# Gate and up of a SwiGLU FFN: blocks without 1/rms, one direct chunk, sums of weights half by accumulating DMAs

## The chip, the cores and the metric

One core of one Trainium2 chip. The metric is the device time of one execution in microseconds (us). TensorE (PE) multiplies, VectorE (DVE) and ScalarE (ACT) work on SBUF and PSUM elementwise, GpSimd (POOL) and SyncE (SP) mostly issue DMAs here. Each engine executes its own instructions in order and waits at semaphores for the others.

## The reference

One layer of a streaming encoder, 512 tokens, D = 1024, float32. Three token mixers run beside each other on one input projection and are merged with gates; then come the output projection, a residual addition, and an FFN of width 2816:

```python
h = rms_norm(x, norm_mix)                      # then mixers, gates, branch projections -> merged
x = x + merged @ w_out
h2 = rms_norm(x, norm_ffn)                     # x * rsqrt(mean(x*x) + 1e-6) * norm_ffn
act = silu(h2 @ w_ffn_gate) * (h2 @ w_ffn_up)  # 1024 -> 2816, twice
x = x + act @ w_ffn_down                       # 2816 -> 1024
```

The change concerns `h2`, gate and up. 1/rms is one factor per token, so it can be multiplied into `h2` or into the results of the two projections.

## The kernel before

**Products in three passes.** Activations lie transposed, channels on the 128 partitions and tokens along the row. Each float32 operand is split into hi and lo: ACT copies it to a rounded type (`whi`, `wh`), DVE subtracts (`wlo`, `wl`). A product is hi x hi + hi x lo + lo x hi, three matmuls. Split tiles of weights come from a pool with three buffers for each name, so a tile's buffer comes free when the product three back has been read. `make_a` prepares the split of a weight tile up to three products ahead.

**Direct chunks.** The first two of the 11 chunks of 256 columns of gate and up (`NDIRECT = 2`) multiply `h2` (all 512 tokens at once) directly: 96 matmuls of 512 columns per chunk. `h2` at that point has norm_ffn's gain but no 1/rms; `rb2`, the vector of 1/rms for all tokens, is multiplied in behind the matmuls. `rms2` computes it, with two matmuls of PE against a matrix of ones (`ps_rms2`).

**Chunks of seven products.** The other nine chunks (`seven`) take the four blocks of `h2` (two halves of the channels, two halves of the tokens) and the four blocks of a chunk's weights, and need seven block products for eight. A product has 24 matmuls of 256 columns. The blocks of `h2` are prepared while the direct chunks run: `norm2` multiplies gain and `rb2` in, `diff_b` makes the differences T1 to T4, `split_b` splits all seven. For each chunk DVE makes four sums of weight blocks (`sums_a`, L1385): S3 = 11 - 21, S2 = 22 - S3, S1 = 21 + 22, S4 = 12 - S2. The products run in `ORDER`, and accumulate in the PSUM tiles Y (`ps_y`) and X (`ps_x`); ACT takes snapshots of the accumulating halves into `tx` and `ty` (L1455). `finish_act` adds the last parts (L1430), takes Silu of the gate half, and multiplies (L1432) into `act`.

**Offsets.** `split_a` lays the first four weight tiles of the stage at the offsets 0, 4, 8 and 12 of their buffers (`STEPS`), all later ones at 16 (`OFF`).

**Down.** The FFN's last projection starts with four direct pieces (`ps_d`, weights `wlo`), then goes on in products of 256 columns into `ps_dy` and `ps_dx`. Its first activation blocks (`Bd11..`, `Bd12..`) are split by `split_d2` in part behind the last gate and up products. Its weights are `wld`: the names at the start of the stage are `wld<-dw` for the first five tiles and `wld<-dr` for the next ones. Some `dw` are sums, made by DMAs of POOL that accumulate in SBUF.

**Order.** A tile scheduler orders each engine's instructions. Some are pinned (`keep_in_program_order`), others moved ahead (`high_priority`).

Of the kernel before, what the change touches and what calls it, by code (L numbers as in the profile page):

```python
# [16 lines left out]
P = 128  # L17
# [12 lines left out]
NDIRECT = 2  # L30
# [37 lines left out]
def layer_kernel(ctx: ExitStack, tc: tile.TileContext, x, xt, vecs, w_in, w_qkv7, w_gate7, w_pool, w_rg, w_ig,  # L68
                 w_branch, w_br7, w_out, w_fg, w_fu, w_fd, w_fd7, out):
# [181 lines left out]
    for c in range(NDIRECT):  # L251
        add_chunk256(("fg", c), w_fg, c * 256)
        add_chunk256(("fu", c), w_fu, c * 256)
# [1002 lines left out]
    with ExitStack() as ffn:  # L1256
# [17 lines left out]
        h2 = []  # L1274
        for c in range(4):
            xr = g4([2, S], f"xr{c}")
            nc.sync.dma_start(xr, xt[2 * c * P:(2 * c + 2) * P, :].rearrange("(j p) t -> p j t", p=P))
            if c == 0:
                psh = [chunk_psum(("out", n), fp) for n in range(2)]
                for half in range(2):  # L1280
                    for n in range(2):
                        half_chunk(psh[n], ("out", n), half, mt, 0, n == half == 0)
            pss = psh[c] if c < 2 else chan_chunk(("out", c), mt, pool=fp)
            hh = g4([2, S], f"h2h{c}", F32R)
            hl = g4([2, S], f"h2l{c}", F32R)
            for j in range(2):
                k = 2 * c + j
                if c % 2 == 0:
                    x1p[c // 2, j] = mp.tile([P, 2, S], F32, tag="m", name=f"x1{c}{j}")
                t = x1p[c // 2, j][:, c % 2, :]  # L1290
                dve.tensor_tensor(t, pss[j], xr[:, j, :], ALU.add)
                x1.append(t)
                gcol = vcol("norm_ffn", k)
                act(hh[:, j, :], t, AF.Copy, scale=gcol)
                dve.scalar_tensor_tensor(hl[:, j, :], t, gcol, hh[:, j, :].bitcast(F32), ALU.mult,
                                         ALU.subtract)
                h2.append((hh[:, j, :], hl[:, j, :]))
                if k == 0:
                    act(sqsum, t, AF.Square)
                else:  # L1300
                    sq = small(f"sq2{k}", 2, "sq2")
                    act(sq, t, AF.Square)
                    dve.tensor_tensor(sqsum, sqsum, sq, ALU.add)

        def rms2():
# [5 lines left out]
            nc.tensor.matmul(ps, onesr, sh, start=True, stop=False)  # L1311
            nc.tensor.matmul(ps, onesr, sl, start=False, stop=True)
# [26 lines left out]
        def split_b(nm, key, which=0):  # L1339
            h, l = g4([4, H], f"B{which}{nm}h", F32R), g4([4, H], f"B{which}{nm}l", F32R)  # L1340
            act(h, BN[key], AF.Copy)
            dve.tensor_tensor(l, BN[key], h.bitcast(F32), ALU.subtract)
            B[which, nm] = h, l

        def diff_b(nm, x, y):
            BN[nm] = corner([4, H], f"hn{nm}")
            dve.tensor_tensor(BN[nm], BN[x], BN[y], ALU.subtract)

        def prepare_b():
            nrm = [lambda k=k: norm2(k) for k in range(8)]  # L1350
            return nrm[:4] + [lambda: split_b("11", (0, 0))] + nrm[4:] + [
                lambda: split_b("21", (1, 0)),
                lambda: diff_b("T1", (0, 1), (0, 0)),
                lambda: diff_b("T2", (1, 1), "T1"),
                lambda: split_b("T2", "T2"),
                lambda: split_b("T1", "T1"),
                lambda: diff_b("T3", (1, 1), (0, 1)),
                lambda: split_b("T3", "T3"),
                lambda: split_b("22", (1, 1)),
                lambda: diff_b("T4", (1, 0), "T2"),  # L1360
                lambda: split_b("T4", "T4")]

        SUMS = {"S2": (("S3", "11", "21", ALU.subtract), ("S2", "22", "S3", ALU.subtract)),
                "S1": (("S1", "21", "22", ALU.add),),
                "S4": (("S4", "12", "S2", ALU.subtract),)}
# [5 lines left out]
        made = [0, NDIRECT]  # L1371
        offs = []

        def load_a(c):
            for nm in ("11", "21", "22", "12"):
                raw[c, nm] = t = corner([2, 4, P], f"w{c}_{nm}")
                for w in range(2):
                    nc.sync.dma_start(t[:, w], cols((w_fg, w_fu)[w], KH[nm] * 4, 4, c * 256 + CH[nm] * P, P))

        def sums_a(c, nm):  # L1380
            for s_, x, y, op in SUMS.get(nm, ()):
                if (c, s_) in raw:
                    continue
                raw[c, s_] = t = wp.tile([P, 2, 4, P], F32, tag="raw", name=f"w{c}_{s_}")
                dve.tensor_tensor(t, raw[c, x], raw[c, y], op)  # L1385

        def make_a(upto):
            while made[0] < min(upto, len(steps)):
                c, nm = steps[made[0]]
                made[0] += 1  # L1390
                if (c, nm) == (NDIRECT, "11"):
                    offs.extend(STEPS)
                while made[1] < min(c + 2, DOWN):
                    load_a(made[1])
                    made[1] += 1
                sums_a(c, nm)
                A[c, nm] = split_a(raw[c, nm], f"{c}_{nm}")
# [30 lines left out]
        def finish_act(t, ps, a):  # L1428

            dve.tensor_tensor(t, t, ps, ALU.add)  # L1430
            act(t[:, 0, :], t[:, 0, :], AF.Silu)
            dve.tensor_tensor(a, t[:, 0, :], t[:, 1, :], ALU.mult)  # L1432


        PRE = ("S2", "S1", "S3")

        def seven(c):
            a = g4([2, S], f"act{c}")
            tx, ty = g4([2, S], f"tx{c}"), g4([2, S], f"ty{c}")
            Y = fp.tile([P, 2, S], F32, tag="mm", name=f"ps_y{c}")  # L1440
            X = fp.tile([P, 2, S], F32, tag="mm", name=f"ps_x{c}")
            lo, hi = slice(0, H), slice(H, S)
            plan = (("11", Y, 1, True, tx, lo, Y, hi),
                    ("12", X, 0, True, None, None, None, None),
                    ("S2", Y, 1, False, tx, hi, Y, hi),
                    ("S1", X, 1, False, ty, hi, X, hi),
                    ("S3", Y, 1, False, ty, lo, Y, hi),
                    ("S4", X, 1, False, None, None, None, None),
                    ("22", Y, 0, False, None, None, None, None))
            n0 = steps.index((c, "11"))  # L1450
            for n, (nm, ps, half, first, t, ts_, src, ss) in enumerate(plan):
                make_a(n0 + n + 3)
                product(A.pop((c, nm)), B[0, WITH[nm]], ps, half, first, True)
                if t is not None:
                    act(t[:, :, ts_], src[:, :, ss], AF.Copy)  # L1455
                if c == DOWN - 1 and nm in PRE:
                    split_d2("11", PRE.index(nm), 0, 0)
                if nm == "S4":
                    finish_act(tx, X, a[:, 0, :])
                if nm == "22":  # L1460
                    finish_act(ty, Y, a[:, 1, :])
            acts.append(a)

        bg.extend([lambda: None, rms2] + prepare_b())
        for c in range(NDIRECT):
            pg = chan_chunk(("fg", c), h2, 3, fp)
            pu = chan_chunk(("fu", c), h2, 3, fp)
            if c == NDIRECT - 1:
                make_a(3)
            a = g4([2, S], f"act{c}")  # L1470
            for j in range(2):
                sg = small(f"sg{c}{j}", 2, "sq2")
                dve.tensor_tensor(sg, pg[j], rb2, ALU.mult)
                act(sg, sg, AF.Silu)
                dve.tensor_tensor(sg, sg, pu[j], ALU.mult)
                dve.tensor_tensor(a[:, j, :], sg, rb2, ALU.mult)
            acts.append(a)
        tick(len(bg))
        for c in range(NDIRECT, NF // 2):
            if c == NF // 2 - 1:  # L1480
                ah, al = g4([2, S], "ah", F32R), g4([2, S], "al", F32R)
# [210 lines left out]
```

## Time and the profile before

| What | Value |
|---|---|
| Time, median of 3 runs | 898.24 us (898.1 to 898.4) |
| The profiled execution | 898.31 us, span 896.5 us |
| Input projection, mixers, branches, to the output projection | 0 to about 524 us |
| Output projection | about 524 to 570.6 us |
| Gate and up | 570.6 to 786.6 us |
| Down | 786.6 to 896 us |
| PE busy | 891.2 us, 99% of the span |
| DVE busy | 739.4 us, 82% |
| ACT busy | 528.5 us, 59% |
| POOL busy | 88.8 us, 10% |
| TensorE clock granted | 9 or more tenths in every slice but the last, 8 |

A row of a timeline gives start, length, engine, line, operation, out<-in, tile shape, and in brackets how long the engine was idle before and what it waited for. A row of groups gives count, busy time, mean ns, and idle time before. Lines of before and after have different numbers for the same place.

### The profile page before, as it was taken

How to read it: one execution, taken by the hardware profiler on the slowest of the kernel's cores; microseconds unless marked ns; L12 is line 12 of the kernel's file. 1: busy time of each engine (PE TensorE's matmuls, PEld its weight loads, DVE VectorE, ACT ScalarE, POOL GpSimd, SP SyncE). 2: the span in 40 equal slices, each digit the busy share in tenths (PEclk: the TensorE clock that was granted, in tenths of full speed). 3: DMA queues.
4: the chain of work that ended last, by engine and by line, in shares of the span. 5: the costliest groups of instructions: out<-in, count | busy, mean ns of one | idle time of the engine just before them, and what ended most of it. 6: DMA issues, size and time to landing. Idle time of an engine off the chain costs nothing.

```text
span 896.5 us, 14227 instructions
## 1 busy us (share of the span) xinstructions
PE 891.2 (99%) x5563; PEld 795.2 (89%) x5563; DVE 739.4 (82%) x934; ACT 528.5 (59%) x730; POOL 88.8 (10%) x130
## 2 busy tenths in 40 slices
PE   9999999999999999999999999999999999999998
PEld 6888778788889888888888988889999999999998
DVE  6897897997786599967887695699988888899974
ACT  6554989546856556554664544545555555746642
POOL 1110002222323101000001100000000000021200
PEclk9999999999999999999999999999999999999999
DMA  9495336798692785734636865336443343897913
GB/s 337 141 297 167 118 114 215 217 302 252 174 276 72 217 252 175 236 108 152 205 90 154 179 190 170 106 107 169 126 131 104 95 118 97 228 243 195 186 42 118
DMA packets 116644, 154.08 MB, mean 172 GB/s; under 512 B 8161, under 2 KB 90081, under 8 KB 116577
## 3 DMA queue, kind: packets, MB, share of 16 engines
q1 hardware_dynamic: 103904, 107.30, 37.8%
q0 software_dynamic: 12528, 45.62, 21.6%
q8 instruction: 43, 0.70, 0.3%
q10 hardware_dynamic: 144, 0.26, 0.1%
q14 instruction: 25, 0.20, 0.1%
HBM read 132.71 MB, written 18.87 MB: 169 GB/s over the span
## 4 chain that ended last, share of the span: by engine, by line
PE 95%; DVE 2%; ACT 2%; issue 1%; DMA 0%; SPq 0%; DVEq 0%; ACTq 0%
PE ps_y L287 11%; PE ps_x L287 8%; PE ps_q L798 7%; PE ps_dy L1611 6%; PE ps_dx L1611 5%; PE ps_br L278 3%; PE ps_br L279 3%; PE ps_br L280 3%; PE ps_bY L1238 2%; PE ps_gate L701 2%; PE ps_gy L287 2%; PE ps_gate L280 2%; PE ps_bX L1238 2%; PE ps_gx L287 2%; PE ps_gate L278 2%; PE ps_gate L279 2%
## 5 line engine op out<-in xcount | busy, mean ns | idle before, releaser
L111 ACT ACTIVATE whi<-raw 128x1024 fp32r<-128x1024 f32 x69 | 73.1, 1060 | 85.2 <-PE ps_out L279 17.9
L112 DVE TENSOR_TENSOR wlo<-raw,whi 128x1024 fp32r<-128x1024 f32 x69 | 84.4, 1223 | 30.7 <-ACT whi L111 30.7
L112 DVE TENSOR_TENSOR wlo<-qw,whi 128x1024 fp32r<-128x1024 f32 x48 | 58.6, 1224 | 22.0 <-ACT whi L111 21.8
L111 ACT ACTIVATE whi<-qw 128x1024 fp32r<-128x1024 f32 x48 | 50.7, 1059 | 33.2 <-PE ps_q L798 15.3
L1403 ACT ACTIVATE wh_S<-w_S 128x1024 fp32r<-128x1024 f32 x36 | 38.3, 1067 | 34.4 <-PE ps_y L287 22.3
L1404 DVE TENSOR_TENSOR wl_S<-w_S,wh_S 128x1024 fp32r<-128x1024 f32 x36 | 43.8, 1222 | 5.2 <-ACT wh_S L1403 5.1
L1515 POOL DMA_DIRECT2D dw<-in_w_down_dram x20 | 16.9, 847 | 313.6 <-DMA dw<-in_w_down_dram 253.2
L1403 ACT ACTIVATE wh<-w 128x1024 fp32r<-128x1024 f32 x27 | 28.8, 1067 | 30.2 <-issue 11.9
L1404 DVE TENSOR_TENSOR wl<-w,wh 128x1024 fp32r<-128x1024 f32 x27 | 33.0, 1222 | 9.9 <-ACT wh L1403 9.9
L1403 ACT ACTIVATE whdS<-dw 128x1024 fp32r<-128x1024 f32 x20 | 21.3, 1067 | 22.5 <-PE ps_dy L1611 11.0
L1404 DVE TENSOR_TENSOR wldS<-dw,whdS 128x1024 fp32r<-128x1024 f32 x20 | 24.3, 1226 | 6.5 <-ACT whdS L1403 6.4
L1054 DVE TENSOR_TENSOR_SCAN E<-K,ahead 128x512 f32<-128x512 f32 (+3 forms) x32 | 25.4, 815 | 4.4 <-ACT K L1050 4.4
L278 PE MATMUL ps_br<-yHH,whi 128*128 128x512 f32 x64 | 25.3, 395 | 0.0
L278 PE MATMUL ps_lru<-HH,whi 128*128 128x512 f32 x64 | 25.2, 394 | 0.0
L278 PE MATMUL ps_br<-yph,whi 128*128 128x512 f32 x64 | 25.2, 394 | 0.0
L278 PE MATMUL ps_pool<-HH,whi 128*128 128x512 f32 x64 | 25.2, 393 | 0.0
L280 PE MATMUL ps_gate<-HH,wlo 128*128 128x512 f32 x64 | 25.0, 391 | 0.0
L278 PE MATMUL ps_gate<-HH,whi 128*128 128x512 f32 x64 | 25.0, 391 | 0.0
L279 PE MATMUL ps_br<-ypl,whi 128*128 128x512 f32 x64 | 25.0, 391 | 0.0
L280 PE MATMUL ps_br<-yph,wlo 128*128 128x512 f32 x64 | 25.0, 391 | 0.0
L279 PE MATMUL ps_br<-yHL,whi 128*128 128x512 f32 x64 | 25.0, 390 | 0.0
L279 PE MATMUL ps_pool<-HL,whi 128*128 128x512 f32 x64 | 25.0, 390 | 0.0
(737 smaller groups left out, 3448.5 us busy)
## 6 DMA issues: line engine op xcount, KB each, us to landing
raw<-in_w_in_dram SPq DMA_DIRECT2D x31, 512.0 KB, 5.3
qw<-in_w_qkv_dram SPq DMA_DIRECT2D x24, 512.0 KB, 7.4
dw<-in_w_down_dram POOLq DMA_DIRECT2D x20, 512.0 KB, 7.5
w<-in_w_ffn_gate_dram SPq DMA_DIRECT2D x36, 256.0 KB, 4.0
w<-in_w_ffn_up_dram SPq DMA_DIRECT2D x36, 256.0 KB, 4.6
raw<-in_w_branch_dram SPq DMA_DIRECT2D x16, 512.0 KB, 4.1
qw<-in_w_qkv_dram POOLq DMA_DIRECT2D x12, 512.0 KB, 7.7
qd<-r POOLq DMA_DIRECT2D x12, 512.0 KB, 7.9
```

Of the source, the lines that this page charges most:

```text
L111: act(hi, raw, AF.Copy)
L112: dve.tensor_tensor(lo, raw, hi.bitcast(F32), ALU.subtract)
L278: nc.tensor.matmul(ps, lh, rh, start=start, stop=False, skip_group_check=skip)
L279: nc.tensor.matmul(ps, lh, rl, start=False, stop=False, skip_group_check=skip)
L280: nc.tensor.matmul(ps, ll, rh, start=False, stop=stop, skip_group_check=skip)
L287: nc.tensor.matmul(o, a_[a][:, w, k, :], b_[b][:, k, :], start=first and n == k == 0, stop=last and n == 2 and k == 3, skip_group_check=True)
L798: nc.tensor.matmul(ps[:, a, :], b_[:, k, ts_], a_[:, kk, :], start=first and n == k == 0, stop=n == 2 and k == 3, skip_group_check=True)
L1054: dve.tensor_tensor_scan(E[:, c0:c0 + n][:, ::-1], K[:, c0 + 1:c0 + n + 1][:, ::-1], ahead[:, S - n:][:, ::-1], 0.0, ALU.mult, ALU.add)
L1238: nc.tensor.matmul(o, ah[x_][:, w, k, :], b[k][y_], start=first_ and n == k == 0, stop=n == 2 and k == 3, skip_group_check=True)
L1403: act(h, src, AF.Copy)
L1404: dve.tensor_tensor(l, src, h.bitcast(F32), ALU.subtract)
L1611: nc.tensor.matmul(o, a_[a][:, w, k0 + k, :], b_[b][:, k, :], start=first and i == k == 0, stop=last and i == 2 and k == nk - 1, skip_grou ...
```

## The change

- `NDIRECT` goes. Chunk 0 is computed on the blocks: four steps 11, 21, 12, 22, each with one weight tile used for both halves of the tokens, 48 matmuls of 256 columns. Ten chunks of seven follow, in the order 11, 12, S1, S2, S4, 22, S3.
- The blocks carry norm_ffn's gain alone (`scale2`, on ACT) and are formed and split in the loop over the four output chunks. Their differences and the other splits stand behind the steps of chunk 0 (`SPREAD`), the differences in place. `rms2` stands behind step (0, "21").
- `finish_act` multiplies both halves of `t` by `rb2`, and one of the two calls has a sign.
- For each chunk of seven, two of four sums are made by accumulating DMAs of POOL (w_21 + 22 and w_11 + 21), two by DVE (S2 = 21 + 11, w_12 + S2). The weights are laid out on the host by blocks, `w_gu7`, so that SP loads a block of 512 KB with one DMA where there were two of 256 KB.

```diff
-        def norm2(k):
+        def scale2(k):
             for j in range(2):
...
-                    b = BN[k // 4, j] = corner([4, H], f"hn{k // 4}{j}")
-                js = slice(j * H, (j + 1) * H)
-                dve.scalar_tensor_tensor(b[:, k % 4, :], x1[k][:, js], vcol("norm_ffn", k),
-                                         rb2[:, js], ALU.mult, ALU.mult)
+                    b = BN[k // 4, j] = g4([4, H], f"hn{k // 4}{j}")
+                act(b[:, k % 4, :], x1[k][:, j * H:(j + 1) * H], AF.Copy, scale=vcol("norm_ffn", k))
...
+        SPREAD = {"11": [lambda: split_b("22", (1, 1)), lambda: diff_b("T1", (0, 0), 1.0, ALU.subtract, (0, 1)),
+                         lambda: split_b("T1", "T1")],
+                  "21": [lambda: diff_b("T2", "T1", -1.0, ALU.subtract, (1, 1)), lambda: split_b("T2", "T2"),
+                         lambda: rms2()],
+                  "12": [lambda: diff_b("T4", "T2", -1.0, ALU.subtract, (1, 0)), lambda: split_b("T4", "T4"),
+                         lambda: diff_b("T3", (0, 1), -1.0, ALU.add, (1, 1))],
+                  "22": []}
+        AORDER = ("11", "12", "S1", "S2", "S4", "22", "S3")
...
-        steps = [(c, nm) for c in range(NDIRECT, DOWN) for nm in ORDER]
+        steps = [(0, nm) for nm in ("11", "21", "12", "22")] + [(c, nm) for c in range(1, DOWN) for nm in AORDER]
...
+                raw[c, nm] = t = (corner if (c, nm) not in early_a else g4)([2, 4, P], f"w{c}_{nm}")
+                nc.sync.dma_start(t, asrc(c, nm))
+                if nm == "21" and c:
+                    nc.gpsimd.dma_start(t, asrc(c, "22"), accum_op=ALU.add)
...
-                if (c, nm) == (NDIRECT, "11"):
+                if (c, nm) == (0, "11"):
                     offs.extend(STEPS)
...
+                src = raw[c, {"S1": "21", "S3": "11", "S4": "12"}.get(nm, nm)]
+                A[c, nm] = split_a(src, f"{c}_{nm}")
+                if nm == "S1":
+                    src = raw[c, "12"]
+                    tc.keep_in_program_order(dve.tensor_tensor(src, src, raw[c, "S2"], ALU.add))
+                if nm == "12" and c:
+                    src = raw[c, "11"]
+                    raw[c, "S2"] = t = wp.tile([P, 2, 4, P], F32, tag="raw", name=f"w{c}_S2")
+                    tc.keep_in_program_order(dve.tensor_tensor(t, raw[c, "21"], src, ALU.add))
+                    nc.gpsimd.dma_start(src, asrc(c, "21"), accum_op=ALU.add)
...
+        def finish_act(t, ps, a, sign):
             dve.tensor_tensor(t, t, ps, ALU.add)
-            act(t[:, 0, :], t[:, 0, :], AF.Silu)
-            dve.tensor_tensor(a, t[:, 0, :], t[:, 1, :], ALU.mult)
+            for w in range(2):
+                dve.tensor_tensor(t[:, w, :], t[:, w, :], rb2, ALU.mult)
+            act(t[:, 0, :], t[:, 0, :], AF.Silu, scale=sign)
+            if sign > 0:
+                dve.tensor_tensor(a, t[:, 0, :], t[:, 1, :], ALU.mult)
+            else:
+                dve.scalar_tensor_tensor(a, t[:, 1, :], sign, t[:, 0, :], ALU.mult, ALU.mult)
...
+            if c == 0:
+                ps, kh = (Y, X)[CH[nm]], KH[nm]
+                w = A.pop((c, nm))
+                for j in range(2):
+                    product(w, B[0, f"{kh + 1}{j + 1}"], ps, j, kh == j == 0, kh == 1)
+                for f in SPREAD[nm]:
+                    f()
...
-        bg.extend([lambda: None, rms2] + prepare_b())
-        for c in range(NDIRECT):
-            pg = chan_chunk(("fg", c), h2, 3, fp)
-            pu = chan_chunk(("fu", c), h2, 3, fp)
```

Two places of DVE's order tell what this moves. The first is a chunk of seven in the middle of the stage. Before, from the addition into `tx` of one chunk (with `ps_x`) on:

```order
687 L1430 TENSOR_TENSOR tx_6051<-tx_6051,ps_x_6054 128x1024
688 L1404 TENSOR_TENSOR wl_12_6251<-w_12_5985,wh_12_6250 128x1024
689 L1432 TENSOR_TENSOR act_6050<-tx_6051 128x512
690 L1430 TENSOR_TENSOR ty_6052<-ty_6052,ps_y_6053 128x1024
691 L1404 TENSOR_TENSOR wl_S_6291<-w_S_6288,wh_S_6290 128x1024
692 L1432 TENSOR_TENSOR act_6050<-ty_6052 128x512
693 L1404 TENSOR_TENSOR wl_S_6322<-w_S_6319,wh_S_6321 128x1024
694 L1385 TENSOR_TENSOR w_S_6378<-w_12_5985,w_S_6288 128x1024
```

And after, from the same addition on, with `rb_5149` for rb2 (`wl_S` is the split of S1, S2, S4 or S3, in the order of the products):

```order
662 L1406 TENSOR_TENSOR tx_6214<-tx_6214,ps_x_6217 128x1024
663 L1380 TENSOR_TENSOR wl_11_6377<-w_11_6142,wh_11_6376 128x1024
664 L1408 TENSOR_TENSOR tx_6214<-tx_6214,rb_5149 128x512 x2
665 L1380 TENSOR_TENSOR wl_12_6405<-w_12_6144,wh_12_6404 128x1024
666 L1411 TENSOR_TENSOR act_6213<-tx_6214 128x512
667 L1372 TENSOR_TENSOR w_S_6408<-w_21_6139,w_11_6142 128x1024
668 L1380 TENSOR_TENSOR wl_S_6447<-w_21_6139,wh_S_6446 128x1024
669 L1406 TENSOR_TENSOR ty_6215<-ty_6215,ps_y_6216 128x1024
670 L1367 TENSOR_TENSOR w_12_6144<-w_12_6144,w_S_6408 128x1024
671 L1408 TENSOR_TENSOR ty_6215<-ty_6215,rb_5149 128x512 x2
672 L1380 TENSOR_TENSOR wl_S_6477<-w_S_6408,wh_S_6476 128x1024
```

Between the end of a chunk (the addition into `ty`) and the split of S2 there now stand a sum of weights and two multiplications by rb2.

The second place is the passage to the down projection. Before:

```order
795 L1430 TENSOR_TENSOR tx_7660<-tx_7660,ps_x_7663 128x1024
796 L112 TENSOR_TENSOR wlo_7898<-raw_7895,whi_7897 128x1024
797 L1432 TENSOR_TENSOR act_7659<-tx_7660 128x512
798 L1430 TENSOR_TENSOR ty_7661<-ty_7661,ps_y_7662 128x1024
799 L1404 TENSOR_TENSOR wld_7927<-dw_7901,whd_7926 128x1024
800 L1432 TENSOR_TENSOR act_7659<-ty_7661 128x512
801 L1580 TENSOR_TENSOR x_5276<-ps_d_7885,x_5276 128x512
```

After:

```order
773 L1406 TENSOR_TENSOR tx_7801<-tx_7801,ps_x_7804 128x1024
774 L111 TENSOR_TENSOR wlo_8040<-raw_8037,whi_8039 128x1024
775 L1408 TENSOR_TENSOR tx_7801<-tx_7801,rb_5149 128x512 x2
776 L1380 TENSOR_TENSOR wld_8069<-dw_8043,whd_8068 128x1024
777 L1411 TENSOR_TENSOR act_7800<-tx_7801 128x512
778 L1406 TENSOR_TENSOR ty_7802<-ty_7802,ps_y_7803 128x1024
779 L1602 TENSOR_TENSOR x_5274<-ps_d_8027,x_5274 128x512
780 L1602 TENSOR_TENSOR x_5281<-ps_d_8027,x_5281 128x512
781 L1401 TENSOR_TENSOR Bd_7994<-act_6669,Bd_7994 128x512
```

The first `wld` has moved from behind the addition into `ty` to ahead of it, and a split of `Bd` from ahead of both to behind them. Further on, all eight additions of `ps_d` to x and the two multiplications of `ty` stand ahead of the second `wld`, which stood behind four of them.

More of the change, by code (lines that the diff above doesn't have):

```diff
@@ L29 @@
 GBUFS = 27
-NDIRECT = 2
 KD = 10
@@ L1273, in layer_kernel @@
         x1 = []
[L1274 to L1303, printed above, removed]
         def rms2():
@@ L1345, in diff_b @@
[L1345 to L1361, printed above, removed]
@@ new lines, in layer_kernel @@
+        T, Z, ah = {}, {}, []
+        for c in range(4):
+            xr = g4([2, S], f"xr{c}")
+            nc.sync.dma_start(xr, xt[2 * c * P:(2 * c + 2) * P, :].rearrange("(j p) t -> p j t", p=P))
+            if c == 0:
+                psh = [chunk_psum(("out", n), fp) for n in range(2)]
+                for half in range(2):
+                    for n in range(2):
+                        half_chunk(psh[n], ("out", n), half, mt, 0, n == half == 0)
+            pss = psh[c] if c < 2 else chan_chunk(("out", c), mt, pool=fp)
+            if c == 1:
+                load_a(0)
+                made[1] = 1
+            if c == 3:
@@ L1469, in layer_kernel @@
                 make_a(3)
-            a = g4([2, S], f"act{c}")
             for j in range(2):
[L1472 to L1481, printed above, removed]
-                act(ah, acts[0], AF.Copy)
-                dve.tensor_tensor(al, acts[0], ah.bitcast(F32), ALU.subtract)
-            seven(c)
+                k = 2 * c + j
@@ L1488, in layer_kernel @@
+            if c == 1:
+                split_b("11", (0, 0))
+                split_b("12", (0, 1))
+            if c > 1:
+                split_b("21", (1, 0), slice(2 * c - 4, 2 * c - 2))
+        for n in range(len(steps)):
+            seven(n)
+        ah, al = ah
         state["stop"] = len(specs)
```

136 lines of the change are left out of this document (78 added, 58 removed).

## The prediction

> **What bounds the kernel now.** I read the page first, then who TensorE (PE) waits for, then the chain of waits by pieces, then VectorE (DVE) and ScalarE (ACT) row by row at the two ends of the changed stage. The page's first part says that PE is busy almost throughout, and the waits of PE over the whole span are three short ones, none in the changed stage:
>
> ```profile
> PE 891.2 (99%) x5563; PEld 795.2 (89%) x5563; DVE 739.4 (82%) x934; ACT 528.5 (59%) x730; POOL 88.8 (10%) x130
> ```
> ```profile
> PE warm_ps L422 <- DVE warm L301: 1.5, 1, 1.5
> PE ps_q L798 <- DVE wlo L112: 0.4, 1, 0.4
> PE ps_gate L701 <- ACT hu L437: 0.3, 1, 0.3
> ```
>
> So a change to this stage can gain only by fewer or quicker matmuls, and can lose wherever a wait of PE appears. Gate and up run from the first ps_fg to the first ps_d, in the timeline of PE:
>
> ```profile
> 570.62 0.39 PE L278 MATMUL ps_fg<-h2h,whi 128*128 128x512 f32 x1
> ...
> 786.60 0.40 PE L278 MATMUL ps_d<-ah,whi 128*128 128x512 f32 x1
> ```
>
> That is 215.98 us, and I call 786.60 "E" below. The chain of waits gives what one matmul costs in it. The columns are start, length and instructions joined:
>
> ```profile
> 585.89 0.23 PE ps_fu L279
> ...
> 594.73 0.23 PE ps_fg L279
> ...
> 614.90 2.87 PE ps_y L287 x24
> 617.77 2.84 PE ps_x L287 x24
> 620.62 2.84 PE ps_y L287 x24
> 623.46 2.83 PE ps_x L287 x24
> 626.28 2.72 PE ps_y L287 x24
> ```
>
> From 585.89 to 594.73 lie 39 matmuls of 512 columns, so one takes 8.84/39 = 0.2267 us, and a direct chunk of 96 takes 21.76 us. A product of 24 matmuls of 256 columns takes 2.72 us (0.1133 each), and a chunk of seven takes 19.04. But the first four products of the stage take 2.87, 2.84, 2.84 and 2.83: these are the four weight tiles that the kernel lays at offsets 0, 4, 8 and 12 of their buffers, before every later one lies at 16. Chunk 2 thus takes 11.38 + 3 x 2.72 = 19.54. Sum before: 2 x 21.76 + 0.45 (the two matmuls of ps_rms2) + 19.54 + 8 x 19.04 = 215.83, against 215.98 seen.
>
> **PE's work after.** Two direct chunks and nine of seven become one chunk on blocks and ten of seven. The block chunk has 4 weight tiles, each used by 48 matmuls of 256 columns. These four tiles now take the offsets 0 to 12, since the list of offsets restarts at (0, "11"). If the slow pace belongs to the tile, the chunk takes 2 x 11.38 = 22.76 and the stage 22.76 + 0.45 + 190.4 = 213.61: **2.2 us less**. If it belongs to the first 11.4 us of the stage, whatever is read, the chunk takes 11.38 + 96 x 0.1133 = 22.26, and the gain is 2.7. I take the tile, since the steps 2.87 to 2.72 fall on tile boundaries, and keep 2.7 for the range.
>
> **The start of the stage.** The blocks' x gain is now an ACT copy, and B11 and B12 are split while the last two output chunks run; B21 and B22 are needed only at the third and fourth quarter. Of what stood between the last output and the first product, the waiting DVE work is an addition of x and the split of a 512-wide half, so I book no wait. PE reads rms2's pair behind step (0, "21"), 11.4 us into the stage. The last DVE input of the pair came here before:
>
> ```profile
> 576.47 0.69 DVE L1309 TENSOR_TENSOR sql<-sqsum,sqh 128x512 fp32r<-128x512 f32 x1 [0.70 <-ACT sqh L1308]
> ```
>
> It was ready 6.5 us into the stage. Two splits of 1024 more stand ahead of it now, 2.3 us, so the cover is some 3 us (2.6 by this). What is at stake if the cover is gone: one split or sum, 0.5 to 1.2 us.
>
> **Steady chunks.** The DVE groups between 640 and 786 give the durations. The timeline of DVE around E gives the pitch, 1.135 for 1024 columns (785.22 to 786.35, 786.95 to 788.09) and 0.60 for 512 (786.35 to 786.95), and with ACT's row there the step from whd to wld, 1.35:
>
> ```profile
> L1404 DVE TENSOR_TENSOR wl_S<-w_S,wh_S 128x1024 fp32r<-128x1024 f32 x30 | 36.6, 1222 | 3.9 <-ACT wh_S L1403 3.9
> L1385 DVE TENSOR_TENSOR w_S<-w,w_S 128x1024 f32<-128x1024 f32 x15 | 18.4, 1225 | 0.5
> L1430 DVE TENSOR_TENSOR tx<-tx,ps_x 128x1024 f32<-128x1024 f32 x8 | 9.8, 1222 | 3.8 <-PE ps_x L287 3.8
> L1432 DVE TENSOR_TENSOR act<-ty 128x512 f32<-128x512 f32 x7 | 4.8, 690 | 0.0
> ```
> ```profile
> 785.22 1.22 DVE L112 TENSOR_TENSOR wlo<-raw,whi 128x1024 fp32r<-128x1024 f32 x1
> 786.35 0.69 DVE L1432 TENSOR_TENSOR act<-tx 128x512 f32<-128x512 f32 x1
> 786.95 1.22 DVE L1430 TENSOR_TENSOR ty<-ty,ps_y 128x1024 f32<-128x1024 f32 x1
> 788.09 1.22 DVE L1404 TENSOR_TENSOR wld<-dw,whd 128x1024 fp32r<-128x1024 f32 x1
> ```
> ```profile
> 786.74 1.06 ACT L1403 ACTIVATE whd<-dw 128x1024 fp32r<-128x1024 f32 x1 [0.71 <-PE ps_y L287]
> ```
>
> Before: 7 splits, 4 sums and 2 additions of 1024, and 2 products of 512, 13 x 1.135 + 2 x 0.60 = 15.96 us of DVE in 19.04. After: two sums go to accumulating DMAs, four multiplications by rb2 come, 11 x 1.135 + 6 x 0.60 = 16.09. DVE's load is the same and stays under PE's. What matters is the order behind the end of a chunk. A weight tile's buffer (three of each) comes free when the product three back ends; ACT then fills wh, and DVE starts wl 1.35 behind ACT's start. For "12" that is 1.4 us before the chunk's end. From there DVE does in order wl_12 1.135, act 0.60, S2 sum 1.135, wl_S1 1.135, ty's addition 1.135, w_12's sum 1.135, rb2 twice 1.20, wl_S2 1.22: 8.7 us, to 7.3 behind the chunk's end. The product S2 starts 3 x 2.72 = 8.16 behind it and reads wl at its third matmul, 8.39. The **margin is 1.1 us in each chunk**; I book nothing, and the rival below uses it up.
>
> The DMAs: SP issues 4 loads of 512 KB per chunk for 8 of 256 KB, and POOL two accumulating ones. Their like stands in the page, and the down stage does the same thing with dw:
>
> ```profile
> qw<-in_w_qkv_dram POOLq DMA_DIRECT2D x12, 512.0 KB, 7.7
> ```
> ```profile
> L1515 POOL DMA_DIRECT2D dw<-in_w_down_dram x20: 841/848/864, 767.2 to 848.0; - x20
> ...
> L1404 DVE TENSOR_TENSOR wldS<-dw,whdS x20: 1218/1226/1234, 822.2 to 872.6; 128x1024 fp32r<-128x1024 f32 x20
> ...
> DMA to landing us min/median/max: 3.5/6.2/11.6
> ```
>
> An accumulation lands some 7.7 us after its issue, at most 11.6 here. w_11's is issued about 2 us behind a chunk's end and read by S3's split some 13 us behind it: 3 us to spare at the median, none at the worst. POOL's issue takes 0.85 us, and DVE's splits beside such issues take 1218 to 1234 ns, no longer than elsewhere. The Trainium skill, "Advanced Engine Details and Errata", section GPSIMD Details, says that Pool shares a read and a write interface with DVE and conflicts with DVE instructions that have two SBUF inputs, which nearly all of these have. By that rule each issue could hold up DVE; the trace of dw does not agree with it, by the 1234 ns.
>
> **The end of the stage.** Here DVE is full. The two windows of the stage's bulk and of the first 25 us of the down stage show DVE at 133.73 of 152.90 and at 23.81 of 25.30:
>
> ```profile
> 633.80:786.70 152.90, 152.90 (x1351) 152.90 (x1350) 133.73 (x125) 88.72 (x110) 3.02 (x4) 1.00 0.46 130
> 786.70:812.00 25.30, 25.30 (x173) 23.41 (x172) 23.81 (x34) 13.42 (x19) 5.47 (x7) 1.00 1.04 232
> ```
>
> The timeline of DVE goes on, and the matmuls of PE behind it tell when the sixth down tile is needed:
>
> ```profile
> 798.91 1.22 DVE L1404 TENSOR_TENSOR wld<-dw,whd 128x1024 fp32r<-128x1024 f32 x1
> 801.61 1.23 DVE L1404 TENSOR_TENSOR wld<-dw,whd 128x1024 fp32r<-128x1024 f32 x1 [1.48 <-ACT whd L1403]
> 802.75 2.49 DVE L1548 SCALAR_TENSOR_TENSOR act<-act 128x512 f32<-128x512 f32 x4
> ...
> 809.89 1.22 DVE L1404 TENSOR_TENSOR wld<-dr,whd 128x1024 fp32r<-128x1024 f32 x1
> ```
> ```profile
> 811.61 0.28 PE L1611 MATMUL ps_dx<-Bd120h,whd 128*128 128x256 f32 x1
> 811.72 0.28 PE L1611 MATMUL ps_dx<-Bd120l,whd 128*128 128x256 f32 x1
> 811.83 0.28 PE L1611 MATMUL ps_dx<-Bd120h,wld 128*128 128x256 f32 x1
> ```
>
> Before, ty's addition starts at E+0.35, the first wld at E+1.49 (its whd had to wait for the last product's buffer, 786.74), and the sixth wld ends at 811.11 = E+24.5, needed at 811.83 = E+25.2. That is a margin of 0.7 with 1.48 us of idle on the way. After, the order puts the first wld ahead of ty's addition. It cannot start before E+1.49 either, so act starts at E+2.62 and ty's addition at E+3.22 instead of E+0.35. From there to the sixth wld the order has: ty's addition 1.135, eight additions of x 4.8, one split that stood ahead before 0.6, rb2 twice 1.2, act as SCALAR_TENSOR_TENSOR 0.66, two pairs of splits and the single one 3.0, four wld 4.54, five SCALAR_TENSOR_TENSOR 3.0, splits, x and splits 3.0: 21.94. The sixth wld then starts at E+25.16 and ends at E+26.38, against E+25.2. PE waits **1.2 us**, and more where an instruction needs the result of the one just ahead, which the pitch leaves out. I take 1.4, between 0.8 and 2.0. What is late next is covered: the idle 1.48 us is not repeated since DVE is behind, and PE's own shift relieves the tiles after it.
>
> **The sum.** The profiled execution took 898.31 (span 896.5 and 1.8 around it), 0.07 above the median of the runs, 898.24. Work -2.2, wait +1.4: -0.8, so **897.5 us**. 0.2% is 1.8 us, about what a measurement of this kernel tells from no change; faster means below 896.4, slower above 900.0.
>
> **Rivals.** *A, no wait at the end of the stage.* For it: the margin is worked out to a few tenths, and one instruction that falls into an earlier gap of DVE takes 0.6 to 1.2 off. Against it: the first wld cannot precede its buffer. The time: 898.31 - 2.2 = 896.1, or 895.6 with the gain of 2.7. *B, slower: DVE is late in every chunk.* The place is wl_S2, three products behind each chunk's end; it decides once the chain grows by more than 1.1 us. If the two POOL issues of a chunk hold DVE up for their 0.85 each, that is 1.7, a wait of 0.6 in each of ten chunks, 897.5 + 6 = 903.5. The Trainium skill's rule above would make the time this. For it: the chain is a row of DVE instructions with no gap. Against it: the 1234 ns beside dw's issues, and the qkv stage, which has twelve such DMAs and makes PE wait once, for 0.4. *C, a wait at the stage's start*: rms2 or B21 late by 0.5 to 1.2 with the forecast's wait, 898.0 to 898.7. *The change does not do what it says*: PE's order shows the block chunk and ten chunks of seven, so that is ruled out.
>
> **How the numbers follow.** Forecast 0.47, A 0.26, B 0.17, C 0.10. Faster by over 0.2% are A and the forecast's edge with the gain of 2.7 and a wait of 0.8 (896.4), together 0.29. Slower are B and a few hundredths of C with a second wait, 0.19. The same: 0.52. The range from 895.5 (A with the gain of 2.7) to 900.8 (a wait of 2.0 for 1.4 and C's 1.2 make 899.3; a quarter of B's 6 comes on top) leaves most of B out, not 2 in 10. The likeliest case alone: 896.4 to 898.2.
>
> **What would show it.** The first four pieces of the stage in the chain at 5.7 us for 48 matmuls; PE's waits with one row for ps_dx on wld of 1.2 to 1.5; no row for ps_y or ps_x on wl. A row for wl_S in every chunk would make B right; a stage shorter by 2.2 with no row for ps_dx, A. I would be wrong in kind if PE's matmuls themselves change pace.

## The result, and the profile after

The changed kernel takes 901.48 us (median of 18 runs, 899.06 to 906.13), the kernel before 898.20 (18 runs, 897.82 to 900.62): slower by 0.39%, ratio 1.0039 with the interval 1.0026 to 1.0051. Forecast were 897.5, in 895.5 to 900.8. The profiled execution took 900.52, with a span of 898.7. Its runs scatter by 7 us where those of before scatter by 3; the profiled one lies 1.0 under their median, and no trace shows what the slower ones lose beyond it.

The chain of the changed kernel at the stage's start (start, length, instructions):

```profile
570.25 5.75 PE ps_y L283 x48
576.00 5.68 PE ps_x L283 x48
581.68 0.47 PE ps_rms L1278 x2
582.14 5.68 PE ps_y L283 x48
587.83 5.66 PE ps_x L283 x48
593.48 2.72 PE ps_y L283 x24
```

The four products of the block chunk take 5.66 to 5.75 us, the slow pace over all 48 matmuls of each, and later ones 2.72 for 24, as forecast. From the first matmul of the stage to the first ps_d the timeline of PE gives 213.63 us:

```profile
570.09 0.28 PE L283 MATMUL ps_y<-B011h,wh 128*128 128x256 f32 x1
...
783.72 0.40 PE L274 MATMUL ps_d<-ah,whi 128*128 128x512 f32 x1
```

Before it was 215.98, so the stage is 2.35 us shorter. From the first ps_d on, 898.7 - 783.7 = 115.0 us are left, where before left 896.5 - 786.6 = 109.9. The loss of 5.1 us lies all in down. PE's waits tell half of it:

```profile
PE ps_dx L1633 <- ACT whd L1379: 1.7, 2, 0.9
PE warm_ps L418 <- DVE warm L297: 1.5, 1, 1.5
PE ps_dx L1633 <- DVE wld L1380: 0.8, 1, 0.8
PE ps_q L794 <- DVE wlo L111: 0.3, 1, 0.3
```

No row for ps_y or ps_x: the steady chunks wait for nothing. The timeline of PE places the three waits for ps_dx:

```profile
809.96 0.51 PE L1633 MATMUL ps_dx<-Bd,whd 128*128 128x256 f32 x2 [0.85 <-ACT whd L1379]
...
818.98 0.39 PE L1633 MATMUL ps_dx<-Bd120h,whd 128*128 128x256 f32 x1 [0.81 <-ACT whd L1379]
...
820.24 0.39 PE L1633 MATMUL ps_dx<-Bd120h,wld 128*128 128x256 f32 x1 [0.76 <-DVE wld L1380]
```

The first is the one forecast, for the sixth down tile. The two others are for the ninth, and the chain says what they end on:

```profile
808.84 1.15 DVE wld L1380
809.99 0.02 SPq L1549
810.01 0.03 issue
810.04 7.72 DMA dr<-in_w_down_dram
...
817.87 1.07 ACT whd L1379
```

The dr tiles have three buffers, so the load of the ninth tile is issued when the sixth is split (808.84 to 809.99). It lands 7.7 us later. Before, the same load was issued at the end of the wld at 809.89, 811.11, and the row in ACT's timeline of the kernel before shows it landed 4.0 us later:

```profile
815.15 1.07 ACT L1403 ACTIVATE whd<-dr 128x1024 fp32r<-128x1024 f32 x1 [2.34 <-DMA dr<-in_w_down_dram]
```

Then the clock: the windows of the changed kernel show it halved behind these waits, in the column before the last two (DMA share and GB/s).

```profile
815.00:818.00 3.00, 3.00 (x29) 2.98 (x27) 0.86 (x2) 0.13 (x1) 0.00 (x0) 1.00 1.02 333
818.00:821.00 3.00, 1.43 (x10) 1.06 (x9) 2.04 (x3) 2.71 (x4) 0.00 (x0) 1.00 0.52 206
821.00:824.00 3.00, 3.00 (x16) 3.00 (x16) 3.00 (x5) 2.82 (x5) 0.00 (x0) 0.50 0.61 175
824.00:827.00 3.00, 3.00 (x27) 3.00 (x26) 3.00 (x4) 1.07 (x1) 0.40 (x1) 0.93 0.48 175
```

PE is busy 1.43 us of 818 to 821, and runs at half clock for the whole of 821 to 824 and by the mean of 0.93 some 0.4 of 824 to 827, 3.4 us, which costs 1.7. Waits of 2.5 and the clock's 1.7 are 4.2 of the 5.1. The rest lies mostly beside the waits: by PE's timeline, from the first ps_dx to the first ps_dy behind it, the same 240 matmuls take 32.07 us (808.71 to 840.78) where they took 27.20 (811.61 to 838.81), so 4.9 of the 5.1 are lost there.

Why the load is slow, the DMA shares (last column but one) tell. Of the changed kernel, in three windows (the columns are PE, PEld, DVE, ACT and POOL busy, clock, DMA share, GB/s):

```profile
795.00:803.00 8.00, 8.00 (x70) 8.00 (x69) 8.00 (x12) 4.79 (x7) 2.33 (x3) 1.00 0.61 114
803.00:812.00 9.00, 8.14 (x70) 7.95 (x70) 9.00 (x13) 5.21 (x7) 1.96 (x3) 1.00 1.03 203
812.00:818.00 6.00, 6.00 (x55) 5.98 (x53) 3.86 (x6) 0.13 (x1) 0.00 (x0) 1.00 1.03 285
```

The same windows of the kernel before:

```profile
795.00:803.00 8.00, 8.00 (x59) 7.55 (x58) 6.51 (x10) 2.13 (x2) 1.67 (x2) 1.00 1.07 216
803.00:812.00 9.00, 9.00 (x80) 9.00 (x79) 9.00 (x14) 5.98 (x9) 1.69 (x2) 1.00 1.01 200
812.00:818.00 6.00, 6.00 (x55) 6.00 (x55) 6.00 (x8) 3.34 (x5) 0.00 (x0) 1.00 0.80 254
```

After, the queues stand partly idle up to 803 and are full up to 818, while the load is in them. POOL's timeline after names what fills them, five accumulations for down from 800.67 on, four of them in a bunch that waited 12.86 us for one load:

```profile
800.67 3.57 POOL L1537 DMA_DIRECT2D dw<-in_w_down_dram  x4 [12.86 <-DMA dw<-in_w_down_dram]
805.53 0.85 POOL L1537 DMA_DIRECT2D dw<-in_w_down_dram  x1 [1.29 <-DVE wld L1380]
```

### The profile page after: what moved, and what is told of

It is laid out like the page before. It is cut to its first block, busy times and chain, and to the rows that moved or that the text cites. A ratio compares the mean times of both kernels' runs of the same rounds, so it can differ in the third digit from the quotient of the medians.

```text
span 898.7 us, 14578 instructions
## 1 busy us (share of the span) xinstructions
PE 891.1 (99%) x5731; PEld 802.4 (89%) x5731; DVE 736.7 (82%) x937; ACT 532.9 (59%) x747; POOL 106.7 (12%) x150
## 4 chain that ended last, share of the span: by engine, by line
PE 93%; DVE 3%; ACT 2%; DMA 1%; issue 1%; DVEq 0%; ACTq 0%; SPq 0%
PE ps_y L283 13%; PE ps_x L283 10%; PE ps_q L794 7%; PE ps_dy L1633 5%; PE ps_dx L1633 4%; PE ps_br L274 3%; PE ps_br L275 3%; PE ps_br L276 3%; PE ps_bY L1234 2%; PE ps_gy L283 2%; PE ps_gate L697 2%; PE ps_gate L276 2%; PE ps_bX L1234 2%; PE ps_gx L283 2%; PE ps_gate L274 2%; PE ps_gate L275 2%
## 5 line engine op out<-in xcount | busy, mean ns | idle before, releaser
L110 ACT ACTIVATE whi<-raw 128x1024 fp32r<-128x1024 f32 x61 | 64.6, 1059 | 73.3 <-PE ps_br L275 14.7
L111 DVE TENSOR_TENSOR wlo<-raw,whi 128x1024 fp32r<-128x1024 f32 x61 | 74.4, 1220 | 28.9 <-ACT whi L110 28.9
L1379 ACT ACTIVATE wh<-w 128x1024 fp32r<-128x1024 f32 x34 | 36.2, 1064 | 49.4 <-PE ps_x L283 24.7
L1380 DVE TENSOR_TENSOR wl<-w,wh 128x1024 fp32r<-128x1024 f32 x34 | 41.6, 1223 | 7.3 <-ACT wh L1379 6.7
L1380 DVE TENSOR_TENSOR wl_S<-w,wh_S 128x1024 fp32r<-128x1024 f32 x30 | 36.6, 1220 | 12.1 <-ACT wh_S L1379 12.0
L1379 ACT ACTIVATE wh_S<-w 128x1024 fp32r<-128x1024 f32 x30 | 31.8, 1060 | 22.5 <-PE ps_y L283 19.8
L276 PE MATMUL ps_br<-yHH,wlo 128*128 128x512 f32 x64 | 25.0, 390 | 0.0
```

The costliest lines, as they stand in the source:

```text
L110: act(hi, raw, AF.Copy)
L111: dve.tensor_tensor(lo, raw, hi.bitcast(F32), ALU.subtract)
L276: nc.tensor.matmul(ps, ll, rh, start=False, stop=stop, skip_group_check=skip)
L1379: act(h, src, AF.Copy)
L1380: dve.tensor_tensor(l, src, h.bitcast(F32), ALU.subtract)
```

## The experiments

Theory D: DVE is late at the passage, and both waits follow from it. Theory Q: the second wait, and with it the half clock, comes from the accumulations that share the queues with the ninth tile's load. All times are medians, beside the kernel before on the same chip, ratios to it.

**Without the multiplications by rb2 in the last chunk.**

```diff
-            for w in range(2):
+            for w in range(2 if len(acts) < DOWN else 0):
                 dve.tensor_tensor(t[:, w, :], t[:, w, :], rb2, ALU.mult)
```

> The changed kernel, with the four multiplications by rb2 left out in the last chunk of gate and up (2.4 us of DVE work at the passage to down; that chunk's output lacks 1/rms). In the changed kernel's trace PE waits 1.05 us for the sixth down tile (wld of the first dr), then 2.2 us for the ninth (whose load is issued only when the sixth is split, at 810.04, and lands 7.7 us later), then runs 3.2 us at half clock. Theory 1 (DVE is late, all else follows): both waits and the slow clock vanish, about 896.2 us. Theory 2 (the load is slow because the DMA queues are crowded by POOL's accumulations issued in a bunch at 800.7): the first wait goes, the second stays at 1 to 2 us since PE comes earlier too, 898 to 900.

Measured: 897.09 (896.0 to 898.96) against 898.42, ratio 0.9987 (0.9977 to 0.9996). PE has no wait in down. That is nearer to theory D, but it moved POOL too: its accumulations started at 797.7, and the ninth tile landed at 814.9. The run doesn't part the theories. The profiled run (898.89) has another loss, at the end of this document.

**The dr tiles in the large pool.**

```diff
-                    DR[nm, n] = t = wp.tile([P, 2, 4, P], F32, tag="raw", name=f"dr{nm}{n}")
+                    DR[nm, n] = t = g4([2, 4, P], f"dr{nm}{n}")
```

> The changed kernel, with the dr tiles of down in the large pool (g4) in place of the three raw buffers, so that their loads need not wait for the split of an earlier dr. DVE's order stays. Theory 1 and 2 both: the first wait of 1.05 us stays, the second goes, and with it the half clock: about 897.2 us. Rival (the half clock has its own cause, or the loads issued earlier crowd the queues for dw): the dip stays, or a new wait for a dw tile appears, 898.5 to 900.

Measured: 899.49 (899.12 to 902.68), ratio 1.0027 (1.0012 to 1.0042). Waits of 1.9 us for wld stayed, without half clock: the expectation missed by 2 us. The edit did not free the loads, since in the large pool they wait for other tiles. The row of the chain is the load of the eighth tile: the changed kernel issued it at 783.79, this run only at 806.27, and in the crowd it was as slow as the ninth's in the changed kernel. PE waited 0.84 us for the sixth tile, 0.49 for the eighth and 0.54 for the ninth, whose load was issued at 808.99 and there by 815.24, but whose split stood in DVE's order behind the eighth's. So the run shows one more slow load in the crowd, and does not test the buffers alone.

```profile
806.27 7.61 DMA dr<-in_w_down_dram
```

**POOL's accumulation of set 2 (the one whose load POOL waited for) behind those that it held up.**

```diff
-            nc.gpsimd.dma_start(buf[n], dsrc(nm, n), accum_op=ALU.add)
+            tc.keep_in_program_order(nc.gpsimd.dma_start(buf[n], dsrc(nm, n), accum_op=ALU.add))
...
-                   lambda: [dadd("22", n, DX) for n in range(5)]] + both("12", 1, 0)[:1])
+                   lambda: [dadd("22", n, DX) for n in (0, 1, 3, 4)]] + both("12", 1, 0)[:1])
...
-                 "12": in_place((0, 0), -1.0, ALU.subtract, (1, 1)) + both("S2", 0, 0),
+                 "12": [lambda f=in_place((0, 0), -1.0, ALU.subtract, (1, 1))[0]: (dadd("22", 2, DX), f())] + in_place((0, 0), -1.0, ALU.subtract, (1, 1))[1:] + both("S2", 0, 0),
```

> The changed kernel with one instruction moved in POOL's queue: the accumulation into dw of set 2 (block 22 onto 21) stands behind the five accumulations 21 onto 11 instead of ahead of four of them; it kept them waiting 12.9 us, to 800.7. Theory 2: the accumulations spread over 797 to 806, the queues are free sooner, the ninth tile's load lands in 4 to 6 us, the second wait shrinks to 0 to 0.5 and the half clock goes: 897.2 to 898. Theory 1 alone: nothing changes, 900 to 901.5.

Measured: 899.35 (897.76 to 901.33), ratio 1.0012 (1.0002 to 1.0021). In the profiled run (897.76) the wait of 0.9 is the only one in down, as theory Q has it, though the ninth tile's load still took some 6 us (issued at 810.29, the tile read from 816.27 on). The median lies 1.6 above that run, and no trace shows why.

**The background work of the first down products spread later.**

```diff
-                    for _ in range(2 - q):
+                    for _ in range((1 + 2 * (q == 1 and p_ == 2)) if nm == "11" else 2 - q):
```

> The changed kernel with the background work of the first down products (in-place sums of act and the splits BdS1) spread later, one item per piece instead of two, so that the split of the sixth down tile stands ahead of seven DVE instructions of 0.6 us; nothing is left out. Theory 1: the sixth wld ends some 3 us earlier, the first wait goes, the ninth load is issued 2 to 3 us earlier and lands in time, 896.0 to 896.5. Theory 2: the first wait goes, the load still takes 7 to 8 us; the second wait is 0 to 1, 896.2 to 898. Rival: the moved work makes a later tile late, 898 or more.

Measured: 902.0 (900.92 to 904.51), ratio 1.0046 (1.0029 to 1.0062). This went against theory D. The sixth tile was in time, and the ninth's load issued at 807.2 in place of 810.0; but POOL's bunch stood where it was (five from 800.31), the ninth tile's whd started at 815.95 and the tenth's at 819.79, and the waits came there, with half clock again. The row of PE's waits in this run:

```profile
PE ps_dx L1633 <- DVE wld L1380: 2.6, 2, 1.9
```

**Offset 16 from the stage's start.**

```diff
-                if (c, nm) == (0, "11"):
-                    offs.extend(STEPS)
```

> The changed kernel, with the first four weight tiles of gate and up at offset 16 like all later ones (no offsets 0, 4, 8, 12 there). Theory O (a matmul's pace goes by its own tile's offset): the four tiles of 48 matmuls run at 113.3 ns in place of 118 to 120, the stage is 1.0 us shorter. Theory S (118 to 120 ns is a state of the sequence of loads and matmuls that starts with the stage, and the steps of the offset bring it out): the whole stage stays at 117 to 120 ns, 1680 matmuls x 4.5 to 6 ns = 7.5 to 10 us longer.

Measured: 899.83 (898.92 to 905.21), ratio 1.0037 (1.002 to 1.0053); the stage from 571.43 to 784.50, 213.07 us, 0.56 shorter. Neither reading of the slow pace, by offset or by place, holds alone. The chain of this run shows the first two products at 5.66 us, the slow pace at offset 16 too, and those behind ps_rms at 5.45:

```profile
571.60 5.66 PE ps_y L283 x48
577.25 5.65 PE ps_x L283 x48
582.90 0.47 PE ps_rms L1278 x2
583.37 5.45 PE ps_y L283 x48
```

**Splits earlier**, alone and with the edits of the third run.

```diff
-        PRE = ("S2", "S4", "22")
+        PRE = ("12", "S1", "S2")
```

> The changed kernel with the splits of act for down's first product (Bd110, Bd111, Bd112) two to three products earlier in the last chunk of gate and up; nothing is left out. DVE has gaps there. By it the first wld and ty's addition come about 0.6 to 1 us earlier, and the second to fourth wld stand ahead of four additions of x. If DVE's lateness and the bunch of accumulations behind the second wld cause the loss: the sixth wld ends 1 to 2 us earlier, POOL's accumulations start at 797 to 798, no wait or one below 0.5 us, 896.3 to 897.5. If the accumulation of set 2 holds POOL anyway (its load lands at 800): the second wait stays, 898.5 to 900.

Measured: 898.81 (896.88 to 901.56), ratio 1.0009 (0.9998 to 1.0021). The wait for the sixth tile is gone; those for the ninth, 1.2 us, stay, though POOL's accumulations ran from 794.3 on: by the chain of this run its load, issued at 809.01, took 7.35.

```profile
809.01 7.35 DMA dr<-in_w_down_dram
```

So an earlier split of the sixth tile does not mend the ninth by itself.

> The same as the one before, with POOL's accumulation of set 2 behind the five of 21 onto 11 as well: the two mends together, nothing left out. Both causes gone: no wait of PE behind 795, no half clock, span 895.7 below the work of before by the 2.2 us of the stage: 896.0 to 896.5, with few runs above 898. If the pace of 117.8 ns that one run showed to its end is independent of both, some runs lie 2 to 3 us higher.

Measured: 899.28 (897.92 to 901.25), ratio 1.0013 (1.0004 to 1.0021). It failed: waits of 1.5 us for the ninth tile, landed 7.65 after its issue. Reordering does not empty the queues.

**The accumulations of 21 onto 11 moved away.** S3 alone needs them, 65 us on. All versions from here on also keep the accumulations in the order in which they are written (the line with `keep_in_program_order` in the third run's diff), which was not run by itself; "earlier splits" is the edit of PRE above. First, alternating with those of S1:

```diff
-                if nm in NEXT:
+                if nm in NEXT and nm != "11":
                     m, buf = NEXT[nm]
                     dadd(m, n, buf)
+                if nm == "S1":
+                    dadd("21", n, DY)
```

> The changed kernel, with the five accumulations of block 21 onto 11 for down, which are needed 65 us after the stage's end, put behind POOL's first accumulation of S1 (some 40 us after it) in place of 800 to 806; nothing is left out, DVE's order stays. Theory Q (the load of the ninth tile takes 7 to 8 us because the queues are full of these accumulations, in before 4.0): it lands 4 to 5 us after its issue at 810, the second wait and the half clock go, the first wait of about 1 us stays: 897.0 to 897.6. Theory D (what counts is when DVE splits the sixth tile): little changes, 899 to 901.

> The one before together with the earlier splits Bd11 (which took the first wait away in its run alone). Theory Q and D together: no wait of PE behind 795: 896.0 to 896.4 if the pace stays 113.3 ns, and faster than before by 0.2%.

Measured: 903.58 (903.36 to 905.04), ratio 1.0056, and with the earlier splits 901.88 (901.57 to 903.11), ratio 1.0042. The times were wrong, the mechanism not: the waits for the ninth tile went in both, but the crowd had moved. An accumulation that S2 needs was issued at 833.29 and landed 17 us later, and PE waited 3.2 and 3.1 us for S2's tiles; a row of the chain of the first:

```profile
833.29 17.25 DMA dw<-in_w_down_dram
```

Next, held on POOL by a copy of one column, with the first two lines of the diff above:

```diff
+                if (nm, n) == ("12", 2):
+                    tk = cst.tile([P, 1], F32, tag="tk", name="tk")
+                    tc.keep_in_program_order(nc.gpsimd.tensor_copy(tk, DA[nm, n][1][:, 0, 0, 0:1].bitcast(F32)))
+                    for n_ in range(5):
+                        dadd("21", n_, DY)
```

> The changed kernel, with the five accumulations of 21 onto 11 for down held on POOL until the eighth down tile is split (a copy of one column of that wld ahead of them), about 812 to 817, in a stretch where the queues stood idle; nothing is left out. Theory Q (the load of the ninth tile is slow because it shares the queues with these accumulations): it lands about 4 us after its issue at 810, the second wait and the half clock go, and unlike with the accumulations at 824 to 834 no wait comes at S2; the first wait of about 1 us stays: 897.0 to 897.6. Theory D (the split of the sixth tile counts alone): 900 to 901.5.

> The one before together with the earlier splits Bd11, which took the first wait away: no wait of PE behind 795, pace 113.3 ns, 896.0 to 896.5, faster than before by 0.2% or a little more. If short waits or the slow pace remain, single runs reach 898.

Measured: 913.4 and 911.66, ratios 1.0165 and 1.0146. The copy took POOL 8.3 us, the accumulations crowded at 828 to 835, and PE waited 6 us for S2's tile. POOL's timeline of the first:

```profile
820.07 8.27 POOL L1568 COPY tk<-wld 128x1 f32<-128x1 f32 x1 [17.92 <-DVE wld L1380]
```

These two runs had also lost some 6 us before the stage, which began at 576.7; what did that, perhaps the four bytes that the new tile takes, was not tried. PE did not wait for the ninth tile in either profile, as in the two runs before, but the times tell only that POOL must not be held so.

Last, behind all five accumulations of S1, again with those two lines, with the earlier splits, without them, and with both the earlier splits and offset 16:

```diff
+                if (nm, n) == ("S1", 4):
+                    for n_ in range(5):
+                        dadd("21", n_, DY)
```

> The changed kernel with the splits Bd11 earlier in gate and up's last chunk, and POOL's five accumulations of 21 onto 11 for down behind all five of S1 (about 837 us in place of 800), so that they neither meet the load of the ninth tile nor hold up those that S2 needs. Nothing is left out. If DVE's lateness and that crowd are the whole loss: no wait of PE behind 795 but perhaps a short one at S3, 896.0 to 896.8, faster than before by 0.2%. If something else is left: above 898.

Measured: 896.04 (895.76 to 896.96) against 898.37, ratio 0.9975 (0.9965 to 0.9984). PE waits nowhere in down.

> The changed kernel with the five accumulations of 21 onto 11 for down behind all five of S1, and nothing else changed (DVE's order as in the changed kernel). If the two causes add up: the first wait of about 0.9 us for the sixth tile stays, the second goes, no half clock: 897.0 to 897.3, 1 us above the version with both mends (896.04). If DVE's lateness makes the ninth load late by itself: 898 or more.

Measured: 897.31 (896.89 to 899.24) against 898.47, ratio 0.9989 (0.9979 to 0.9999), with one wait in down, of 0.9 for the sixth tile, in PE's waits of this run:

```profile
PE ps_dx L1636 <- ACT whd L1379: 0.9, 1, 0.9
```

The queues in its windows, to set beside those above:

```profile
795.00:803.00 8.00, 8.00 (x69) 7.96 (x68) 8.00 (x12) 4.48 (x6) 1.21 (x2) 1.00 1.03 189
803.00:812.00 9.00, 8.14 (x71) 7.95 (x70) 9.00 (x13) 5.62 (x8) 0.00 (x0) 1.00 0.11 19
812.00:818.00 6.00, 6.00 (x55) 6.00 (x55) 6.00 (x10) 3.84 (x6) 0.00 (x0) 1.00 0.77 246
```

DVE is full over the whole of 795 to 818 there, and PE's busy time in 803 to 812 is the same 8.14 as in the changed kernel. Only the queues differ, 0.11 for 1.03, and the second wait and the half clock are gone. The ninth tile's load, issued at 810.47, had landed when ACT reached the tile, at most 3.5 us later:

```profile
813.93 1.07 ACT L1379 ACTIVATE whd<-dr 128x1024 fp32r<-128x1024 f32 x1 [3.52 <-DVE wld L1380]
```

Four versions make the two shares plain (medians in us; the kernel before took 898.14 to 898.47 beside them, and the right column has the pinned order of POOL as well):

| | accumulations as changed | behind S1's |
|---|---|---|
| splits as changed | 901.48 | 897.31 |
| splits earlier | 898.81 | 896.04 |

With DVE's order as changed, the crowd costs 4.2 us (4.5 by the ratios to the kernel before); without the crowd, DVE's lateness costs 1.3. The two don't simply add: with the earlier splits the crowd costs 2.8 (3.1 by the ratios), because the second wait is shorter and no half clock showed in that profile.

> The one before, with the first four tiles of gate and up at offset 16 as well, which in its run alone made the stage 0.56 us shorter (213.07 for 213.63): 0.5 us below the one before.

Measured: 895.78 (895.29 to 897.22) against 898.37, ratio 0.9973 (0.9962 to 0.9983). It is the fastest version run, and beats both kernels by more than 0.2%; its lead of 0.26 over the one without the offsets is within the scatter of their runs.

## Why the prediction was wrong

- **PE's work after**: right in its number. The slow pace belongs to the tile as far as the step of 48 matmuls goes (5.66 to 5.75 against the 5.66 to 5.74 worked out), and the stage took 213.63 for 213.61. The number is in part luck: in the run at offset 16 the first two products were as slow without the steps of the offset, so the pace does not go by them alone.
- **The start of the stage**: right, no wait. Rival C fell.
- **Steady chunks**: right. DVE's timeline of the changed kernel has a chunk's wl_S2, and the chain the product that reads it:

```profile
770.62 1.22 DVE L1380 TENSOR_TENSOR wl_S<-w_S,wh_S 128x1024 fp32r<-128x1024 f32 x1
```
```profile
773.00 2.72 PE ps_y L283 x24
```

It ended at 771.84 and was read at the third matmul, 773.23: a margin of 1.4, for 1.1. POOL's issues held nothing up; by the groups of the changed kernel DVE's wl took 1223 ns on average, and rival B fell. By the Trainium skill, "Advanced Engine Details and Errata", GPSIMD Details, Pool conflicts with DVE instructions that have two SBUF inputs; no row of this stage shows it:

```profile
L1380 DVE TENSOR_TENSOR wl<-w,wh 128x1024 fp32r<-128x1024 f32 x34 | 41.6, 1223 | 7.3 <-ACT wh L1379 6.7
```

- **The end of the stage**: the mechanism was right, its size near. The sixth wld ended at 809.98, E+26.3 with E at 783.72, for E+26.38; PE waited 0.85 us by the view for 1.2 to 1.4. Rival A fell.
- **What is late next**: this step failed. "PE's own shift relieves the tiles after it" looked at DVE alone. The sixth tile's split also releases the buffer for the ninth tile's load; the prediction said of each queue only how long an accumulation takes, and did not follow POOL's queue into down. There POOL waits in each kernel for a load that SP issues when a buffer of the large pool comes free. SP's queue and POOL in the timeline of the kernel before:

```profile
784.34 0.86 SPq L1512 DMA_DIRECT2D dw<-in_w_down_dram  x2
```
```profile
794.04 1.79 POOL L1515 DMA_DIRECT2D dw<-in_w_down_dram  x2 [3.59 <-DMA dw<-in_w_down_dram]
```

  SP's of the changed kernel, beside POOL's row at 800.67 above:

```profile
784.17 0.90 SPq L1534 DMA_DIRECT2D dw<-in_w_down_dram  x2
```

  Against E that is E-2.3 before and E+0.4 after for the load, and E+7.4 and E+17 for POOL: of the 9.5 us that POOL is later, 2.7 come from the issue and the rest from a slower landing. Three accumulations that POOL had issued from 784.32 to 787 shared the queues with that load; in the version with the accumulations behind S1's and POOL's order pinned, POOL issued none between 780.7 and 793.6, and had the load at 793.64. In the changed kernel the accumulations behind it then shared the queues with the ninth tile's load, which took 7.7 us. The accumulating DMAs of the change itself did no harm in the stage; those of down did, which the diff does not touch.
- **The sum**: taken alone, the terms that were worked out give 897.5, and the version without the crowd took 897.31. The missed term is some 4 us.
- **Bounds**: the range ended at 900.8, from C and a quarter of B. No rival ended in down's loads.

## What to carry to other kernels

When a change makes an engine late at a passage, follow what its late instruction releases, buffers and DMA issues too, and look at the queues' share there: here a load that met a share of 1.0 landed 3 to 4 us later. A DMA in a queue that waits for one late load holds all behind it and sends them off in a bunch. Transfers that are needed tens of microseconds later belong behind those that are needed next, and not merely ahead of their own deadline.

## What the runs showed of the hardware

PE's granted clock fell to 0.50 for some 3.4 us after 1.57 us without matmuls in the 3 us before, and did not after a single wait of 0.85, nor after 1.43 us without matmuls between 818 and 821 in the run with both the earlier splits and set 2 behind the five. The Trainium skill, "TensorE: Matmul & The Clock Gate", "Part 1: The HAM clock gate", tells of a fall after an idle window of about 3.4 us; here 1.57 us, less than half of that, were enough.

The pace of 256-column matmuls has a second value, 117.8 ns for 113.3, that isn't bound to an offset. In the profiled run of the kernel without rb2's last multiplications, it set in at 820 with no wait in the view and stayed to the end; the chain's rows of 240 and 120 matmuls are 3 to 4% longer than the 27.20 and 13.60 of the others:

```profile
809.24 27.93 PE ps_dx L1633 x240
837.17 28.27 PE ps_dy L1633 x240
865.44 14.13 PE ps_dx L1633 x120
```

The rows of the chain behind 809 are 2.9 us longer by it in sum, and the run lies 2.5 to 2.9 us over the three fastest of the same kernel (896.0 to 896.4). What starts it, and what ended it behind ps_rms at offset 16, stays open.
